# One attention layer with a feed-forward block on one core: two accumulation groups in one PSUM tile, group norm over 512 columns, and a due time for every instruction of the plan

## The chip, the core and the metric

The kernel runs on one core of one Trainium2 chip, in one launch, all in float32. The metric is device time in microseconds. Of the kernel before, three runs are known: 1293.23, 1293.79 and 1300.29 us, median 1293.79 us. TensorE is PE in the profile (PEld is its loading of weights), VectorE is DVE, ScalarE is ACT, GpSimd is POOL, and SP is the engine whose queue issues nearly all DMAs.

## The reference, cut to what matters

One layer on 1024 tokens of width 1024. Four mixers of 256 columns each write the 16 groups of 64 columns; then a norm per group, the output projection and a gated feed-forward block.

```python
def hybrid_layer(x, ...):
    hn = rms_norm(x, g_mix)
    proj = hn @ w_in
    ...
    o_a = nsa_mixer(qa, kca, vca, ksa, vsa, kwa, vwa, gta, b_gate, ...)
    o_b = short_conv_mixer(cvb, cvc, cvu, conv_w).reshape(b, s, CONV_CH // HEAD_DIM, HEAD_DIM)
    o_c = stick_breaking_attention(to_heads(qc, N_HEADS_C), to_heads(kc, N_HEADS_C), to_heads(vc, N_HEADS_C))
    ...
    for window, dil in DILATED_CONFIGS:
        o_i, lse_i = dilated_attention(qdh, kdh, vdh, window, dil, slopes_d)
    ...
    groups = jnp.concatenate([o_a, o_b, o_c, o_d], axis=2)
    groups = rms_norm(groups, g_out.reshape(N_GROUPS, HEAD_DIM)).reshape(b, s, MIX_WIDTH)
    x = x + groups @ w_out
    h2 = rms_norm(x, g_ffn)
    return x + (jax.nn.silu(h2 @ w_gate) * (h2 @ w_up)) @ w_down
```

## The kernel before

Every float32 operand is split into a rounded part and a rest (names ending in h and l, `whi` and `wlo`), and each product is three float32r matmuls (`mm3`, lines 241 to 243): high by high, high by low, low by high.

**Stages.** Input norm, transposes and the first projections; then, as the list `ORDER` names them, the three-branch attention `attn_nsa` for two pairs of heads (`n0`, `n1`), the convolutions (`c0`, `c1`), stick-breaking attention (`proj_stick`, `attn_stick`: `ps`, `s`) and dilated attention (`proj_dil`, `attn_dil`: `pd`, `d`) for two pairs of heads each, the gains (`g`), the output projection (`out_half`), the second norm (`ln2`), and the feed-forward block with Strassen-Winograd products: seven products a step for gate and up (`winograd`, lines 1054 to 1056), then seven for the down projection (lines 241 to 243 with `hw`). In the trace the input norm and the first projections fill the time to some 100 us, attention and projections that to 600 us, gate and up 636 to 1074 us.

**What the change touches.** Attention takes 128 queries of both heads of a pair (`attn_nsa`, tile `qt`), or 256 queries of one head at a time (`pv_heads`, pair `qp`). The weights of a score tile are transposed on PE into a bank `Tp` (line 570), copied by ACT (`pth`, line 558), their rest taken by DVE (`ptl`, line 559), and multiplied with the values on PE into a bank `Op` (lines 575, 576, 694, 695). `Op` holds 512 columns, of which one head or one query tile uses 256. `o_evac` moves it out: ACT copies 64 of its partitions (line 580), DVE adds the other 64 into the tile `MO` (line 582). When `MO` has 256 columns, `finish` norms them: squares (ACT, line 593), their rounded part (ACT, 605) and rest (POOL, 607), two matmuls that sum the squares of each group (PE, 606 and 608), Ln and Exp (ACT, 609 and 610) and the product (DVE, 611); then `MO` is stored (line 617), or, for the last pair of heads, split with its gain (`gain`, lines 819 and 820) into `MH` and `ML`, which `out_half` multiplies.

**Projections beside them.** `v_T` copies a finished projection out of its bank (ACT, `vraw`, line 367) and transposes it on PE (line 370). `normed` copies projections into `raw` (ACT, line 357), scales them (DVE, line 299) and lets PE transpose them (line 343). `q_split` and `k_split` write the halves of queries and keys (lines 311, 312, 319, 321).

**What sets the order.** The kernel is built twice. After the first time a planner (`make_plan`, `_traced`, `_planned`) goes through the instructions like a list scheduler: at each engine, of those that are ready it takes the one with the lowest number, where the number is the place in the program less a lead. Leads come from two tables, `EARLIER` by kind of tile and `LEADS` by group and stage (some 500 entries). The second time the instructions get the planned order on each engine (`fix_order`) and each tile the planned buffer. The plan reaches up to the first use of the pool `f2`, that is to the down projection. Of PSUM's eight banks three are `PR`, two `T`, two `SP`, one `O`; gate and up use all eight in turn (`PF`).

## Time and profile before

| | |
|---|---|
| median of three runs | 1293.79 us |
| the profiled execution, its own time | 1296.53 us |
| its span, first to last instruction | 1294.5 us |
| busy: PE, PEld | 1270.6 us (98%), 1088.3 us (84%) |
| busy: DVE, ACT, POOL | 972.0 us (75%), 701.5 us (54%), 652.2 us (50%) |
| mean granted clock of PE | 0.997 |

The profiled execution took 2.7 us more than the median; 2.0 us of its time lie around the span. A busy PE in this profile is a matmul between its start and a modelled end, and matmuls overlap, so the busy share alone does not say how fast PE goes: the distance from one start to the next does.

### The profile page before, as it was taken

The numbers are of one execution on the slowest core, as the hardware profiler recorded it, in microseconds if no ns is written. First come the engines' busy times: TensorE is split into PE (matmuls) and PEld (weight loads), VectorE is DVE, ScalarE is ACT, GpSimd is POOL, SyncE is SP. The second block draws the span as 40 slices with busy tenths as digits, with TensorE's granted clock in tenths as the row PEclk, the third lists the DMA queues.
The fourth block names the chain that finished last, engine by engine and source line by source line (L and its number), as shares of the span: only waits on it lengthen the run. The fifth ranks groups of instructions, "written<-read, shape, count | busy, mean of one in ns | idle before, by whom it ended". The sixth has DMA issues, their size and how long they took to land.

```text
span 1294.5 us, 20254 instructions
## 1 busy us (share of the span) xinstructions
PE 1270.6 (98%) x7041; PEld 1088.3 (84%) x7041; DVE 972.0 (75%) x1793; ACT 701.5 (54%) x1437; POOL 652.2 (50%) x490
## 2 busy tenths in 40 slices
PE   8999999999999999999999999999999999999998
PEld 8988888888889798999888888888888888887886
DVE  6758878789888979754688896776576667599862
ACT  6557686778889878456553323333232335423540
POOL 6354364445546534434773444444444435565655
PEclk9999999999999999999999999999999999999999
DMA  6340030211111315543554444323313339852534
GB/s 238 110 131 1 9 105 10 61 53 44 55 47 32 97 26 191 165 148 105 194 177 146 155 161 149 123 85 119 122 65 117 103 106 355 277 181 65 146 100 153
DMA packets 90550, 153.04 MB, mean 118 GB/s; under 512 B 10128, under 2 KB 35728, under 8 KB 90448
## 3 DMA queue, kind: packets, MB, share of 16 engines
q1 hardware_dynamic: 89888, 149.92, 36.0%
q0 software_dynamic: 560, 1.84, 0.4%
q8 instruction: 55, 0.90, 0.3%
q14 instruction: 47, 0.39, 0.1%
HBM read 111.08 MB, written 36.44 MB: 114 GB/s over the span
## 4 chain that ended last, share of the span: by engine, by line
PE 59%; DVE 5%; issue 1%; DMA 0%; ACT 0%; POOL 0%; SPq 0%; DVEq 0%; ACTq 0%
PE PRp L241 6%; PE PRp L243 6%; PE PRp L242 6%; PE PRp L1054 4%; PE PRp L1055 4%; PE PRp L1056 4%; PE Tp L1054 2%; PE SPp L1054 2%; PE Tp L1055 2%; PE Tp L1056 2%; PE SPp L1056 2%; PE SPp L1055 2%; DVE bB L1033 2%; PE Tp L570 1%; DVE fw L1114 1%; PE Op L1054 1%
## 5 line engine op out<-in xcount | busy, mean ns | idle before, releaser
L108 POOL TENSOR_TENSOR wlo<-raw,whi 128x512 fp32r<-128x512 f32 x94 | 124.8, 1336 | 102.2 <-ACT whi L107 74.4
L1043 POOL TENSOR_TENSOR fw<-fraw,fw 128x512 fp32r<-128x512 f32 x50 | 71.0, 1421 | 144.4 <-ACT fw L1042 135.4
L559 DVE TENSOR_TENSOR ptl<-Tp,pth 128x512 fp32r<-128x512 f32 (+2 forms) x172 | 102.1, 606 | 25.3 <-ACT pth L558 23.3
L558 ACT ACTIVATE pth<-Tp 128x512 fp32r<-128x512 f32 (+2 forms) x172 | 89.6, 531 | 54.2 <-PE Op L575 24.0
L1114 DVE TENSOR_TENSOR fw<-sraw,fw 128x512 fp32r<-128x512 f32 x73 | 90.5, 1255 | 34.5 <-ACT fw L1113 34.3
L1042 ACT ACTIVATE fw<-fs 128x512 fp32r<-128x512 f32 x88 | 52.0, 629 | 108.2 <-DVE fs L1033 74.1
L1114 POOL TENSOR_TENSOR hw<-bB,hw 128x512 fp32r<-128x512 f32 x55 | 80.8, 1481 | 50.1 <-ACT hw L1113 49.5
L241 PE MATMUL PRp<-XH,whi 128*128 128x512 f32 x224 | 91.4, 408 | 0.0
L242 PE MATMUL PRp<-XL,whi 128*128 128x512 f32 x224 | 90.1, 402 | 0.0
L243 PE MATMUL PRp<-XH,wlo 128*128 128x512 f32 x224 | 89.9, 402 | 0.1
L570 PE MATMUL Tp<-ident,S 128*128 128x128 f32 x552 | 87.6, 273 | 0.0
L1043 DVE TENSOR_TENSOR fw<-fs,fw 128x512 fp32r<-128x512 f32 x88 | 75.1, 880 | 7.6 <-ACT fw L1042 7.5
L107 ACT ACTIVATE whi<-raw 128x512 fp32r<-128x512 f32 x102 | 63.2, 620 | 31.4 <-PE PRp L242 9.3
L651 POOL TENSOR_SCALAR S<-S,ll 128x640 f32<-128x640 f32 (+7 forms) x32 | 53.6, 1675 | 51.9 <-DVE ll L649 30.9
L1042 ACT ACTIVATE fw<-fraw 128x512 fp32r<-128x512 f32 x50 | 31.5, 630 | 84.1 <-DMA fraw<-in_wup_dram 26.3
L570 PEld LDWEIGHTS Tp<-ident,S 128*128 128x128 f32 x552 | 66.6, 140 | 8.3 <-DVE ptl L559 0.2
L241 PE MATMUL PRp<-whi,MH 128*128 128x256 f32 (+1 forms) x248 | 72.0, 293 | 0.9 <-DVE VD L374 0.8
L242 PE MATMUL PRp<-wlo,MH 128*128 128x256 f32 (+1 forms) x248 | 70.9, 287 | 0.0
L243 PE MATMUL PRp<-whi,ML 128*128 128x256 f32 (+1 forms) x248 | 70.6, 287 | 0.0
L1113 ACT ACTIVATE hw<-bB 128x512 fp32r<-128x512 f32 x62 | 38.9, 628 | 49.9 <-PE Op L243 21.2
L1033 DVE TENSOR_TENSOR fs<-fraw 128x512 f32<-128x512 f32 x44 | 42.1, 956 | 31.9 <-DMA fraw<-in_wgate_dram 18.3
L793 POOL TENSOR_TENSOR S<-S,R 128x128 f32<-128x128 f32 (+7 forms) x32 | 47.3, 1483 | 35.7 <-DVE R L791 28.6
(481 smaller groups left out, 4467.5 us busy)
## 6 DMA issues: line engine op xcount, KB each, us to landing
fraw<-in_wgate_dram SPq DMA_DIRECT2D x22, 512.0 KB, 4.2
fraw<-in_wup_dram SPq DMA_DIRECT2D x22, 512.0 KB, 4.1
bB<-in_wdown_dram SPq DMA_DIRECT2D x44, 256.0 KB, 4.5
sraw<-hS SPq DMA_DIRECT2D x44, 256.0 KB, 2.7
raw<-in_wout_dram SPq DMA_DIRECT2D x30, 256.0 KB, 2.8
hS<-s SPq DMA_DIRECT2D x30, 256.0 KB, 2.0
sraw<-hA SPq DMA_DIRECT2D x29, 256.0 KB, 3.6
xt<-in_x_dram SPq DMA_DIRECT2D x8, 512.0 KB, 9.5
```

What stands on the lines that cost most here:

```text
L108: (lo or nc.gpsimd).tensor_tensor(dst_lo, raw, f(dst_hi), op=OP.subtract)
L241: nc.tensor.matmul(ps, a[0], b[0], start=first, stop=False)
L242: nc.tensor.matmul(ps, a[0], b[1], start=False, stop=False)
L243: nc.tensor.matmul(ps, a[1], b[0], start=False, stop=last)
L558: nc.scalar.activation(ph[:, c], tp[:, :n], AF.Copy)
L559: nc.vector.tensor_tensor(pl[:, c], tp[:, :n], f(ph[:, c]), op=OP.subtract)
L570: nc.tensor.transpose(tp[:, i * 128:(i + 1) * 128], p, ident)
L1043: eng.tensor_tensor(wt[:, 1, :], a, f(wt[:, 0, :]), op=OP.subtract)
L1054: nc.tensor.matmul(ps, wt[:, 0, c], bh[:, k, :], start=k == 0, stop=False)
L1055: nc.tensor.matmul(ps, wt[:, 0, c], bl[:, k, :], start=False, stop=False)
L1056: nc.tensor.matmul(ps, wt[:, 1, c], bh[:, k, :], start=False, stop=k == 3)
L1114: eng.tensor_tensor(wt[:, 1, :], raw, f(wt[:, 0, :]), op=OP.subtract)
```

## The change

Two heads (`pv_heads`) or two query tiles (`attn_nsa`) now share one `Op` tile, with `c0` or `oc` as the column where each begins; only the first matmul in the tile carries the flag that starts an accumulation. `o_evac` copies 512 columns once. `MO` holds 512 columns, and `finish` runs once for 512. The temporary of `o_evac` and `finish` (`otmp`) is one buffer of 512 columns where it was two of 256. `EARLIER` and `LEADS` are gone: a table `DUE` gives each of the 9372 planned instructions a number of its own, and the planner takes the ready instruction with the lowest.

```diff
-    def pv(o, items, first=True, last=True):
+    def pv(o, items, first=True, last=True, c0=0):
...
-                nc.tensor.matmul(o[:, 256 - b:256], v, ph[:, c], start=first and g + i == 0, stop=False)
-                nc.tensor.matmul(o[:, 256 - b:256], v, pl[:, c], start=False, stop=last and g + i == n - 1)
+                nc.tensor.matmul(o[:, c0 + 256 - b:c0 + 256], v, ph[:, c], start=first and g + i == 0, stop=False)
+                nc.tensor.matmul(o[:, c0 + 256 - b:c0 + 256], v, pl[:, c], start=False, stop=last and g + i == n - 1)
 
     def o_evac(o, writes):
-        tmp = sm.tile([128, 256], F32, tag="otmp", bufs=2, name="otmp")
-        nc.scalar.activation(tmp[64:128, :], o[64:128, :256], AF.Copy)
-        for dst, c0, c1 in writes:
-            nc.vector.tensor_tensor(dst, o[0:64, c0:c1], tmp[64:128, c0:c1], op=OP.add)
+        tmp = otmp("ok")
+        nc.scalar.activation(tmp[64:128, :], o[64:128, :], AF.Copy)
+        for dst, at in writes:
+            nc.vector.tensor_tensor(dst, at(o)[0:64], at(tmp)[64:128], op=OP.add)
+
+    def otmp(name):
+        return sm.tile([128, 512], F32, tag="otmp", bufs=1, name=name)
 
     def mixtile():
-        return sm.tile([128, 256], F32, tag="MO", bufs=2, name="MO")
+        return sm.tile([128, 512], F32, tag="MO", bufs=2, name="MO")
...
         for qt in range(NT):
+            if qt % 4 == 0:
+                MO = mixtile()
             if qt % 2 == 0:
-                MO = mixtile()
+                o = Ot()
+            oc = qt % 2 * 256
...
             if qt % 2:
-                finish(hp, qt * 128 - 128, 256, MO, tk())
+                mv = MO[:, qt % 4 * 128 - 128:qt % 4 * 128 + 128].rearrange("p (j n) -> p j n", n=128)
+                o_evac(o, [(mv[h * 64:(h + 1) * 64], lambda z, h=h: z.rearrange("p (j g n) -> p j g n", j=2, g=2)[:, :, h, :])
+                           for h in range(2)])
+            if qt % 4 == 3:
+                finish(hp, qt * 128 - 384, 512, MO, otmp("fk"))
...
     def pv_heads(P, V, qp, k8):
-        MO = mixtile()
+        if qp % 2 == 0:
+            MIX["o"] = mixtile()
+        MO = MIX["o"]
+        o = Ot()
         for h in range(2):
-            o = Ot()
...
-            pv(o, items)
-            o_evac(o, [(MO[h * 64:(h + 1) * 64, :], 0, 256)])
-        finish(k8, qp * 256, 256, MO, tk())
+            pv(o, items, first=h == 0, last=h == 1, c0=h * 256)
+        mc = slice(qp % 2 * 256, qp % 2 * 256 + 256)
+        o_evac(o, [(MO[h * 64:(h + 1) * 64, mc], lambda z, h=h: z[:, h * 256:h * 256 + 256]) for h in range(2)])
+        if qp % 2:
+            finish(k8, qp * 256 - 256, 512, MO, otmp("fk"))
...
-EARLIER = {"evac": 1000, "split": 400, "fill": -30, "T": 0, "SP": 10, "O": 150}
-LEADS = {
-    "ACT B22 B": -649,
...
+DUE = """
+-15229 98 85 94 562 -9495 -117 269 -399 538 -348 185 -252 -78 -17 159 -192 37 587 -462 238 51 -277 439 -255 447
...
-        op.lead = sum(EARLIER[k] for k in op.kinds)
-        if acc:
-            op.lead += LEADS.get(op.group, 0) + LEADS.get(op.stage, 0)
...
+    due = list(accumulate(map(int, DUE.split())))
+    due += range(10 ** 8, 10 ** 8 + n - len(due))
...
-                heappush(now[e], (i - ops[i].lead, i))
+                heappush(now[e], (due[i], i))
```

The order on PE, first around the values' projection of the second pair of heads in stick-breaking attention. `PRp` is the projection's bank, `vraw` its copy by ACT, which lines 370 transpose; before:

```order
L242 MATMUL PRp_5876<-XL_139,whi_5872 128x512
L243 MATMUL PRp_5876<-XH_138,wlo_5873 128x512
L241 MATMUL PRp_5876<-XH_138,whi_5872 128x512
L242 MATMUL PRp_5876<-XL_139,whi_5872 128x512
L243 MATMUL PRp_5876<-XH_138,wlo_5873 128x512
L370 MATMUL PRp_5903<-ident_77,vraw_5901 128x128 x4
L522 MATMUL SPp_5427<-ckl_4771,cql_4769 128x512
L524 MATMUL SPp_5427<-ckr_4772,zq_4196 128x512
L241 MATMUL PRp_5910<-XH_140,whi_5866 128x512
```

The transposes stand right behind the projection whose copy they read. The same place now (`PRp_5727` takes the part of `PRp_5903`):

```order
L576 MATMUL Op_5125<-ptl_5183,VC_4637 128x256
L575 MATMUL Op_5125<-pth_5182,VC_4637 128x256
L522 MATMUL SPp_5798<-dkh_5396,dqh_5394 128x128
L576 MATMUL Op_5125<-ptl_5183,VC_4637 128x256
L524 MATMUL SPp_5798<-dkr_5398,zq_4098 128x128
L570 MATMUL Tp_5275<-ident_77,S_5206 128x128
L370 MATMUL PRp_5727<-ident_77,vraw_5725 128x128
L241 MATMUL PRp_5734<-XH_140,whi_5690 128x512
L370 MATMUL PRp_5727<-ident_77,vraw_5725 128x128 x3
```

Products with the values, scores and a transpose were moved in between. Next the group norm of the last store, where dilated attention's first pair of heads ends and the output projection runs beside it (`PRp` from `MH`, `ML`); `pth` and `ptl` are the two parts of the squares. Before:

```order
L241 MATMUL PRp_7563<-whi_7553,MH_6853 128x256
L242 MATMUL PRp_7563<-wlo_7554,MH_6853 128x256
L243 MATMUL PRp_7563<-whi_7553,ML_6854 128x256
L606 MATMUL Tp_6465<-pth_6466,blk1r_130 128x256
L608 MATMUL Tp_6465<-ptl_6467,blk1r_130 128x256
L522 MATMUL SPp_7115<-dkh_6478,dqh_6476 128x512
```

Now (the two matmuls are lines 609 and 611):

```order
L609 MATMUL Tp_6249<-pth_6250,blk1r_130 128x512
L241 MATMUL PRp_7328<-whi_7289,MH_6637 128x256
L241 MATMUL PRp_7351<-whi_7283,MH_6637 128x256
L242 MATMUL PRp_7351<-wlo_7284,MH_6637 128x256
L243 MATMUL PRp_7351<-whi_7283,ML_6638 128x256
L241 MATMUL PRp_7351<-whi_7283,MH_6637 128x256
L242 MATMUL PRp_7351<-wlo_7284,MH_6637 128x256
L522 MATMUL SPp_6879<-dkl_6263,dql_6261 128x512
L524 MATMUL SPp_6879<-dkr_6264,zq_4098 128x512
L242 MATMUL PRp_7328<-wlo_7290,MH_6637 128x256
L611 MATMUL Tp_6249<-ptl_6251,blk1r_130 128x512
```

Nine matmuls stand between the two of the norm, where none stood. Last a place in gate and up, where `PRp_9341` takes the bank that `PRp_9147` leaves, once DVE has read it. Now:

```order
L1065 MATMUL PRp_9147<-B22_8403,fw_9144 128x512
L1066 MATMUL PRp_9147<-B22_8403,fw_9144 128x512
L1064 MATMUL Op_9290<-T4_8402,fw_9287 128x512
L1065 MATMUL Op_9290<-T4_8402,fw_9287 128x512
L1064 MATMUL PRp_9324<-T2_8400,fw_9321 128x512
L1066 MATMUL Op_9290<-T4_8402,fw_9287 128x512
L1064 MATMUL Op_9290<-T4_8402,fw_9287 128x512
L1064 MATMUL PRp_9341<-T1_8399,fw_9338 128x512
```

Before, at such a place (`PRp_9405` takes the bank of `PRp_9238`, whose last matmul stands 69 rows further up, and none of the rows between writes that bank):

```order
L1054 MATMUL PRp_9386<-T3_8659,fw_9383 128x512
L1055 MATMUL PRp_9386<-T3_8659,fw_9383 128x512
L1056 MATMUL PRp_9386<-T3_8659,fw_9383 128x512
L1054 MATMUL PRp_9405<-B22_8661,fw_9402 128x512
L1055 MATMUL PRp_9405<-B22_8661,fw_9402 128x512
```

Five matmuls stand between the last in a bank and the first of the next tile in it. Over gate and up the order has 136 such turns; the fewest matmuls in one were 36 before, and now ten turns have nine or fewer. Bank `O` in attention turns 24 times instead of 48; the fewest matmuls in a turn are 17 now and were 9.

## Rows read from the trace of the kernel before

**Rows 1.** From the page: busy time, share of the span and instructions of each engine.

```profile
PE 1270.6 (98%) x7041; PEld 1088.3 (84%) x7041; DVE 972.0 (75%) x1793; ACT 701.5 (54%) x1437; POOL 652.2 (50%) x490
```

**Rows 2.** Busy time of each engine in stretches of the span; the first number is the length of the stretch, the numbers in brackets count instructions, then the granted clock, the DMA share and GB/s.

```profile
400.00:450.00 50.00, 46.25 (x317) 41.12 (x316) 47.12 (x78) 43.38 (x81) 30.41 (x17) 1.00 0.27 74
...
500.00:550.00 50.00, 46.56 (x353) 43.81 (x352) 39.20 (x93) 31.17 (x70) 25.30 (x19) 1.00 0.44 134
...
630.00:1090.00 460.00, 459.96 (x1996) 370.92 (x1996) 342.82 (x428) 171.40 (x303) 213.44 (x152) 1.00 0.42 141
1090.00:1200.00 110.00, 108.48 (x458) 86.72 (x457) 91.47 (x90) 44.11 (x79) 64.49 (x41) 0.98 0.58 187
```

**Rows 3.** The same view for two short stretches with matmuls of 256 columns and one with 512 columns alone.

```profile
82.60:86.19 3.59, 3.59 (x17) 3.59 (x18) 3.25 (x9) 2.93 (x7) 2.20 (x2) 0.54 0.26 75
86.35:88.87 2.52, 2.52 (x23) 2.52 (x22) 1.13 (x3) 0.38 (x1) 2.52 (x3) 1.00 0.36 104
700.00:800.00 100.00, 100.00 (x430) 80.50 (x429) 83.96 (x104) 34.47 (x60) 45.35 (x30) 1.00 0.48 163
```

**Rows 4.** For whom PE waited between 110 and 600 us, the whole list: total us, times, longest.

```profile
PE PRp L370 <- ACT vraw L367: 2.3, 4, 0.7
PE SPp L522 <- DVE dql L312: 1.6, 1, 1.6
PE Tp L608 <- POOL ptl L607: 1.4, 2, 0.8
PE PRp L241 <- DVE VD L374: 1.1, 2, 0.8
PE PRp L241 <- ACT raw L357: 0.8, 1, 0.8
PE SPp L522 <- DVE S L785: 0.8, 1, 0.8
PE SPp L522 <- PE PRp L243: 0.5, 1, 0.5
PE Op L576 <- DVE ptl L559: 0.5, 2, 0.3
PE PRp L606 <- ACT sh L605: 0.4, 1, 0.4
```

**Rows 5.** PE's instructions in order of time around one of these waits: start, duration, and in brackets the idle time before.

```profile
361.86 0.39 PE L243 MATMUL PRp<-XH,wlo 128*128 128x512 f32 x1
362.94 0.66 PE L370 MATMUL PRp<-ident,vraw 128*128 128x128 f32 x4 [0.69 <-ACT vraw L367]
```

**Rows 6.** The same view around a group norm and behind it.

```profile
515.50 0.38 PE L606 MATMUL Tp<-pth,blk1r 128*128 128x256 f32 x1
516.72 0.39 PE L608 MATMUL Tp<-ptl,blk1r 128*128 128x256 f32 x1 [0.84 <-POOL ptl L607]
...
520.16 0.28 PE L243 MATMUL PRp<-whi,ML 128*128 128x256 f32 x1
522.03 0.47 PE L522 MATMUL SPp<-dkl,dql 128*128 128x512 f32 x1 [1.59 <-DVE dql L312]
```

**Rows 7.** ACT's groups of instructions: out<-in, shape, count, busy us, mean ns.

```profile
L580 ACT ACTIVATE otmp<-Op 64x256 f32<-64x256 f32 x48 | 18.3, 380 | 15.4 <-PE Op L576 14.3
...
L609 ACT ACTIVATE tk<-Tp,epst 128x256 f32<-128x256 f32 x24 | 11.3, 471 | 4.1 <-PE Tp L608 3.8
...
L610 ACT ACTIVATE tk<-tk 128x256 f32<-128x256 f32 x24 | 9.9, 414 | 0.3
...
L593 ACT ACTIVATE tk<-MO 128x256 f32<-128x256 f32 x24 | 9.8, 409 | 6.8 <-DVE MO L582 6.7
...
L294 ACT ACTIVATE sq<-raw 128x512 f32<-128x512 f32 x12 | 7.5, 628 | 0.9 <-PE Tp L343 0.8
...
L311 ACT ACTIVATE dql<-PRp,gsc 64x512 fp32r<-64x512 f32 x4 | 2.7, 683 | 0.1
L609 ACT ACTIVATE yc<-PRp,epst 128x512 f32<-128x512 f32 x4 | 2.7, 682 | 0.1
```

**Rows 8.** DVE's groups, in the same columns.

```profile
L1043 DVE TENSOR_TENSOR fw<-fs,fw 128x512 fp32r<-128x512 f32 x88 | 75.1, 880 | 7.6 <-ACT fw L1042 7.5
L559 DVE TENSOR_TENSOR ptl<-Tp,pth 128x512 fp32r<-128x512 f32 x104 | 70.5, 688 | 21.1 <-ACT pth L558 19.7 <-PE Op L575 0.3 <-PE SPp L522 0.2
...
L582 DVE TENSOR_TENSOR MO<-Op,otmp 64x256 f32<-64x256 f32 x32 | 13.4, 417 | 5.3 <-ACT otmp L580 4.3
...
L1033 DVE TENSOR_TENSOR u<-Tp,u 128x512 f32<-128x512 f32 x18 | 12.4, 690 | 19.9 <-PE Tp L1056 17.7 <-POOL p L1033 2.0
...
L611 DVE TENSOR_TENSOR MO<-MO,tk 128x256 f32<-128x256 f32 x24 | 10.3, 429 | 2.8 <-ACT tk L610 2.8
...
L582 DVE TENSOR_TENSOR MO<-Op,otmp 64x128 f32<-64x128 f32 x32 | 9.1, 284 | 1.1 <-ACT otmp L580 0.2
```

**Rows 9.** The chain of work that ended last, from 433 to 440 us: start, us, what.

```profile
433.67 4.25 DVE R L791
...
439.47 0.39 PE PRp L241
```

**Rows 10.** PE's instruction at the start of the slow stretch of rows 3, in the columns of rows 5.

```profile
82.60 0.39 PE L241 MATMUL PRp<-wa,XH 128*128 128x256 f32 x1 [1.15 <-ACT raw L357]
```

**Rows 11.** For whom SP's queue of DMAs waited, one row of the list: total us, times, longest.

```profile
SPq L617 <- DVE MO L611: 97.6, 11, 35.4
```

More of the change, by code (lines that the diff above doesn't have):

```diff
@@ L621, in flush_stores @@
             nc.sync.dma_start(*stores.pop(0))
-    def tk():
-        return sm.tile([128, 256], F32, tag="otmp", bufs=2, name="tk")
     def attn_nsa(hp, Q):
@@ L693, in attn_nsa @@
             ph, pl = evac_T(tp, 256)
[L694 to L695 removed]
+            nc.tensor.matmul(o[:, oc:oc + 256], vcHL, ph[:, :256], start=qt % 2 == 0, stop=False)
+            nc.tensor.matmul(o[:, oc:oc + 256], vcHL, pl[:, :256], start=False, stop=False)
             five = [(j0, 384, 384), (j0 + 384, 256, 256)]
[L697 removed]
+            pv(o, branch(1, ks, five if CK and qt == 4 else chunks(0, L), False, False), first=False, last=False, c0=oc)
             wch = chunks(0, L) if qt < 4 else five
[L699 to L701 removed]
+            pv(o, branch(2, kw, wch, qt >= 4, False), first=False, last=qt % 2 == 1, c0=oc)
             if qt % 2:
[L703 removed]
+                mv = MO[:, qt % 4 * 128 - 128:qt % 4 * 128 + 128].rearrange("p (j n) -> p j n", n=128)
[3 more added lines that the diff above has]
+                finish(hp, qt * 128 - 384, 512, MO, otmp("fk"))
+    MIX = {}
     def pv_heads(P, V, qp, k8):
[L706 removed]
+        if qp % 2 == 0:
+            MIX["o"] = mixtile()
+        MO = MIX["o"]
+        o = Ot()
         for h in range(2):
[L708 removed]
             items = []
@@ L1235 @@
 PE_RATE = 0.92
[L1236 removed]
+REUSES = {"sd": ("sa",), "bp": ("sm", "sa", "sd"), "lp": ("sm", "sa", "sd"), "lq": ("sm", "sa", "sd"), "b2": ("lq",)}
 PINNED_UNTIL = "f2"
[L1238 to L1764 removed]
@@ L1767, in _size @@
+DUE = """
[302 rows of a table added]
+"""
 def _size(ap):
@@ L1946, in _planned @@
     from heapq import heappush, heappop
+    from itertools import accumulate
     n = len(ops)
```

532 lines of the change are left out of this document (removed), and 301 rows, old and new, of the table DUE.

## The prediction

> **What bounds the kernel now.** I first read the page's busy times: PE is busy 1270.6 us of the span [rows 1]. Since a busy PE need not be a PE at its pace, I next read the stretches. Gate and up hold 430 matmuls of 512 columns in 100.00 us [rows 3]: one every 0.2326 us, and over 460 us no idle time worth a number [rows 2]. There is nothing to win in that third of the time, only to lose. Attention is different: PE is idle 3.75 us between 400 and 450 and 3.44 between 500 and 550, where DVE is busy 47.12 and 39.20 of 50 us [rows 2]. The list of PE's waits says for whom [rows 4]: 15 waits, 9.4 us, on copies by ACT (`vraw`, `raw`), on the rest of the squares by POOL, on DVE.
>
> The view undercounts. From the matmul at 361.86 to the transpose at 362.94 pass 1.08 us, of which 0.2326 are the matmul's pace; 0.85 is lost, and the view shows 0.69 [rows 5]. The missing 0.16 is what a matmul is shown beyond its pace (0.39 against 0.23 us). So the 15 waits lose 9.4 + 15 x 0.16 = 11.8 us, and a wait under 0.16 us isn't in the list at all. Last I read the chain: at 433.67 it lies 4.25 us in DVE's scan `R`, and goes through DVE until PE goes on at 439.47 [rows 9]. PE's waits there end with DVE's queue.
>
> So the end is set by PE's work, which the change leaves as it is (24 norm matmuls fewer, each of twice the columns), plus PE's waits in attention. The gain can only come out of those, 11.8 us and the short ones.
>
> **Copies and norms, part by part.** ACT: the copy out of `Op` was 48 x 0.380 us = 18.2; now 24 of 64x512, by the row of that shape 0.683 each, 16.4. A norm was 0.409 twice (the square; the rounding is of that shape too) + 0.471 + 0.414 = 1.70 us on ACT, 24 times, 40.9; now 12 times 0.628 (square, rounding and, as the nearest row, Exp) x 3 + 0.682 (Ln) = 2.57, together 30.8 [rows 7]. ACT gets 11.9 us back. DVE: the 32 adds of 64x128 at 0.284 become 16 at 0.417, 9.1 to 6.7; the 24 norm products of 0.429 become 12 of 512 columns, between 0.688 and 0.880 by the nearest rows, 10.3 to 8.3 or 10.6 [rows 8]. DVE gets 2.1 to 4.4 us back. Neither engine is the bound on average, so these microseconds count only where PE waits for that engine.
>
> The single `otmp` adds a dependence: the copy out of the next `Op` tile waits until the norm before it is through with its temporary. Behind that copy ACT's later copies `pth` would be queued, and PE waits for those. I cost it at nothing: the norm's chain on ACT, DVE and POOL is some 4 us, and now a whole `Op` tile of two heads or two query tiles is filled before the next copy is due. If that cover is gone, it costs what is left of those 4 us at up to 12 norms.
>
> Bank `O` now waits for one copy of 0.683 and two adds of 0.417, 1.5 us, 24 times, before it was 0.380 + 0.417 = 0.8, 48 times [rows 7, 8]. The whole list of PE's waits has no `otmp` and no `MO` [rows 4], so this move was covered; the order now has at least 17 matmuls in such a turn, where it had 9. Cost 0. The Trainium skill speaks against this part (Perfetto Trace Analysis, Matmuls): independent groups should rotate through different banks so that moving one out overlaps the next one's matmuls. By that rule, uncovered, one bank for both heads would add 24 x 1.5 = 36 us. The trace doesn't agree: one bank turned 48 times without a wait of PE's, since PE has projections to do meanwhile; I give that case no chance of its own.
>
> SP: 20 stores of `MO` become 10 of twice the size. Its queue stood 97.6 us behind such stores [rows 11], with loads queued after them. There are half as many of them now, and PE waited for no load in attention [rows 4]: cost 0; a load that came late would stand among PE's waits or DVE's.
>
> **The order, wait by wait.** Each wait of rows 4 with its hidden 0.16, and what the new order does there (PE work between two rows of the order is counted at the paces of rows 3):
> - `vraw`: 2.3 + 4 x 0.16 = 2.9 us. Five of the eight copies had under 0.6 us of PE work between projection and transposes (none at the first place shown); now one has none, one has 0.7 and six more than that. One wait of 0.85 stays: gain 2.1.
> - `ptl` of the norm (line 608): 1.4 + 0.3 = 1.7. At 515.50 and 516.72 the two matmuls stood one behind the other, 1.2 us apart [rows 6]; now nine stand between. Gain 1.7.
> - `VD`: 1.1 + 0.3 = 1.4. PE work between grows from 0.6 and 1.1 us to 1.5 and 2.4. Gain 1.4.
> - `raw`: 0.8 + 0.16 = 1.0. From none and 0.4 us of work to 0.7 and 0.8. Gain 0.8.
> - `dql`: 1.6 + 0.16 = 1.8, at 520.16 to 522.03 [rows 6]. It came last in a full DVE queue. The score no longer stands so close, but that queue is no shorter in the new order. Half: 0.9.
> - `S`, `PRp`, the other `ptl` and `sh`: 2.2 + 0.8 = 3.0 us. For `S` the order has the same few matmuls; I leave the others too.
>
> Together 6.9 us.
>
> **Short waits.** No row shows them. At least nothing goes; at most PE gets every microsecond that ACT and DVE save, 11.9 + 4.4 = 16.3. The chain in the bad stretch runs over DVE [rows 9], so the nearest rows are DVE's: its saving of 2.1 to 4.4. I take 3.0.
>
> **Gate and up.** Ten turns of a bank now have nine matmuls or fewer in between, five in the case shown; 36 was the least. After the last matmul DVE has to read the bank: 0.16 + 0.690 = 0.85 us, and five matmuls last 1.16. If DVE is free at that moment, nothing is lost; if it has just begun a rest `fw` (0.880) [rows 8], PE waits 0.85 + 0.88 - 1.16 = 0.57. So 0 to 5.7 us for ten. Below nothing it cannot go, PE has no wait to lose there [rows 2]. DVE has been idle before such reads (17.7 us in front of 18 of them [rows 8]), so I take the low side: 1.1. The queue behind a late DVE is its own next rests, for which PE has a stock of weights.
>
> The down projection keeps its order; its stall and slow clock in 1090 to 1200 (1.52 us idle, clock 0.98 [rows 2]) stay.
>
> **Sum.** -6.9 - 3.0 + 1.1 = -8.8 us. Against the profiled execution's own time 1296.5 - 8.8 = 1287.7; the median stands 2.7 us lower, so 1285.0.
>
> **Rivals.**
> - *The waits only change their place*: DVE binds. For it: DVE at 47.12 of 50 us [rows 2], the chain over the scans, only 2.1 to 4.4 us of relief; in the new order two pairs of scores near the end of attention follow a pair with hardly a matmul between, though they want a bank that DVE must read. Against it: 8 of the 15 waits are on ACT and POOL, where the relief is. The 3.0 of short waits don't come and half of the 6.9 comes back: 1296.5 - 3.5 + 1.1 - 2.7 = 1291.4, between 1288 and 1298.
> - *Slower through gate and up*: a late DVE at the tight turns delays PE, and since PE is at 100% there every delay stays. At 0.57 us each it doesn't decide; it does from about 1.5 us each over the ten, where DVE is two instructions late. PE's clock then adds to it: at 82.60, after an idle time of 1.15 us, the granted clock is 0.54 on average, 17 matmuls take 3.59 us, where 23 take 2.52 afterwards (1.2 against 2.4 GHz) [rows 3, 10]; that cost 3.59 - 17 x 0.11 = 1.7 us. Ten turns at 1.5 and four such stretches are 15 + 7 = 22: 1296.5 - 9.9 + 22 - 2.7 = 1305.9. Against it: at 522.03 PE had idled 1.59 us and the clock of that stretch stayed 1.00 [rows 2, 6]. The Trainium skill (TensorE: Matmul & The Clock Gate, HAM oscillation) says that an engine that idles falls back to the lower clock; the trace agrees at 82.60 and not at 522.03.
> - *All of it comes*: the margins in the order do away with the 3.0 that I leave and with more short waits, 6 to 9 us of them. 1296.5 - 9.9 - 9 + 0 - 2.7 = 1274.9.
>
> **How the numbers follow.** My forecast (gain 5 to 14 us, 1280 to 1288.5) has 0.45, all of it 0.15, changed places 0.28, slower through gate and up 0.12. A difference under 0.5%, 6.5 us, can't be told from none: faster means below 1287.3, slower above 1300.3. Faster: 0.38 of the first, 0.15 of the second, 0.53. Same: 0.07 of the first, 0.28 of the third and 0.02 of the fourth, which need not reach its whole price: 0.37. Slower 0.10. The range runs from 1275, where the second case ends, to 1298, the upper end of the third; outside lie most of the fourth and a tail below, under 0.2.
>
> **What would show it.** In the profile of the changed kernel: the list of PE's waits between 110 and 600 us without `ptl` of the norm and `VD` and with one or two `vraw`, its total from 9.4 to under 5; idle time of PE in 400 to 550 well under 7.3 us; in gate and up 430 matmuls in 100 us still, or fewer if the turns are late, with waits of PE for DVE `u`; ACT's time down by some 12 us, DVE's by 2 to 4. I am wrong if the waits in attention go and the time doesn't: then it was lost in gate and up or in waits too short for the view; and if the same sum of waits stands under other names, DVE was the bound.

## The result, and the profile after

The changed kernel takes 1283.11 us (median of five runs, 1281.58 to 1285.18); beside it the kernel before took 1294.98 (five runs). The ratio is 0.990, with a 95% interval of 0.9875 to 0.9929: the kernel got faster by 11.9 us, about 1%. The forecast was 1285.0. The profiled execution took 1281.58 us, with a span of 1279.7; that of before 1296.53 with 1294.5, so the two traces differ by 14.8 us.

The page first: busy time, share of the span and instructions of each engine, as in [rows 1].

```profile
PE 1263.0 (99%) x7017; PEld 1081.8 (85%) x7017; DVE 961.7 (75%) x1763; ACT 689.2 (54%) x1363; POOL 655.4 (51%) x478
```

PE has the same columns to go through, in 24 matmuls fewer. ACT has 12.3 us less work, DVE 10.3 less.

Where the 14.8 us went is read from the starts of three matmuls: the first of gate and up's seven-product steps (line 1054, now 1064), the first of the down projection (with `hw`), and the last. Some plain products of gate and up stand ahead of the first border, from 636.68 us before and 624.42 after; they take 48.3 and 48.4 us, so they have no part in the gain. PE's instructions in order of time, in the columns of [rows 5], before:

```profile
684.98 0.40 PE L1054 MATMUL PRp<-T,fw 128*128 128x512 f32 x1
...
1082.26 0.40 PE L241 MATMUL PRp<-hw,fw 128*128 128x512 f32 x1
...
1189.94 0.49 PE L241 MATMUL Tp<-hw,fw 128*128 128x512 f32 x1 [0.41 <-ACT hw L1113]
1191.55 0.50 PE L242 MATMUL Tp<-hw,fw 128*128 128x512 f32 x1 [1.11 <-POOL hw L1114]
...
1290.02 0.40 PE L243 MATMUL Tp<-hw,fw 128*128 128x512 f32 x1
```

The same view after (the first two rows belong to an experiment below):

```profile
401.43 0.50 PE L609 MATMUL Tp<-pth,blk1r 128*128 128x512 f32 x1 [0.39 <-ACT pth L608]
...
402.40 0.39 PE L241 MATMUL PRp<-whi,XH 128*128 128x256 f32 x1
...
672.82 0.50 PE L1064 MATMUL PRp<-T,fw 128*128 128x512 f32 x1 [0.19 <-ACT fw L1052]
...
1070.42 0.40 PE L241 MATMUL PRp<-hw,fw 128*128 128x512 f32 x1
...
1178.63 0.50 PE L242 MATMUL Tp<-hw,fw 128*128 128x512 f32 x1 [0.71 <-POOL hw L1124]
...
1275.57 0.39 PE L243 MATMUL Tp<-hw,fw 128*128 128x512 f32 x1
```

| stretch | before | after | difference |
|---|---|---|---|
| start to gate and up's steps | 684.98 | 672.82 | -12.2 |
| gate and up's steps, to the down projection | 397.28 | 397.60 | +0.3 |
| down projection, to the last matmul's start | 207.76 | 205.15 | -2.6 |
| the end | 4.5 | 4.1 | -0.4 |

Part of this, in two places, is the granted clock. The windows of the kernel before, in the columns of [rows 2], with the stretch of attention up to 400 us on top:

```profile
100.00:400.00 300.00, 297.06 (x1844) 260.43 (x1843) 249.99 (x724) 234.61 (x540) 151.53 (x120) 1.00 0.15 42
...
82.87:86.28 3.41, 3.41 (x18) 3.41 (x18) 3.07 (x8) 2.66 (x7) 2.29 (x2) 0.50 0.28 79
1192.20:1195.61 3.41, 3.41 (x10) 2.63 (x9) 3.41 (x3) 1.90 (x4) 3.41 (x3) 0.50 0.26 77
```

and after:

```profile
100.00:400.00 300.00, 299.73 (x1888) 264.96 (x1887) 257.84 (x718) 233.70 (x511) 155.34 (x117) 1.00 0.15 42
400.00:450.00 50.00, 48.77 (x342) 43.94 (x340) 42.36 (x83) 41.28 (x75) 27.86 (x14) 1.00 0.28 79
...
500.00:550.00 50.00, 47.60 (x369) 44.83 (x368) 44.14 (x103) 32.28 (x62) 18.68 (x14) 1.00 0.49 156
630.00:1090.00 460.00, 459.81 (x1989) 370.04 (x1988) 329.44 (x418) 173.79 (x303) 216.91 (x150) 1.00 0.41 141
...
82.51:86.10 3.59, 3.59 (x30) 3.59 (x31) 3.49 (x9) 3.08 (x9) 2.77 (x2) 1.00 0.23 73
```

Before, the clock stood at its lower level, 1.2 GHz, for 3.41 us at 82.87 and again at 1192.20; each cost 3.41 x 0.5 = 1.7 us. After, there is none: at 82.51 PE starts 30 matmuls in 3.59 us, where it started 17 [rows 3]. So of the 12.2 us ahead of gate and up 1.7 are clock and 10.5 are work, and of the 2.6 us in the down projection 1.7 are clock and 0.9 a shorter stall: there the weights `hw` came late for two matmuls in a row, now for one. Traces of one and the same order in that stage differ by up to 0.7 (experiment 5), so these 0.9 are hardly more than chance. In their clock the two profiled executions differ by more than the two kernels do: over the 66 runs of before that were taken beside the experiments the mean granted clock is 0.9981, over the five runs of after 0.9992. By that some 0.0011 x 1290 = 1.4 us of the 11.9 are clock, an estimate.

In attention PE's idle time fell from 3.75 to 1.23 us between 400 and 450, and from 3.44 to 2.40 between 500 and 550 [rows 2]. For whom PE waited between 110 and 600 us, the whole list after the change, in the columns of [rows 4]:

```profile
PE PRp L243 <- DVE ML L830: 0.7, 1, 0.7
PE PRp L241 <- DVE dkr L321: 0.7, 1, 0.7
PE Tp L570 <- DVE S L766: 0.7, 1, 0.7
PE PRp L370 <- ACT vraw L367: 0.7, 1, 0.7
PE Tp L570 <- DVE ptl L559: 0.6, 2, 0.4
PE SPp L522 <- DVE mm L549: 0.5, 1, 0.5
PE Tp L609 <- ACT pth L608: 0.4, 1, 0.4
```

Eight waits, 4.3 us, where 15 took 9.4. The norm's `ptl`, `VD`, `raw` and `dql` are gone, `vraw` is down from four to one. The last windows show something else: between 100 and 400 us DVE did 249.99 us of work before and 257.84 after, and between 400 and 450 it is busy for 42.36 us where it was for 47.12 [rows 2].

The wide instructions after the change, ACT's and then DVE's groups, in the columns of [rows 7, 8]:

```profile
L580 ACT ACTIVATE ok<-Op 64x512 f32<-64x512 f32 x24 | 14.2, 593 | 10.7 <-PE Op L576 10.3
L612 ACT ACTIVATE fk<-Tp,epst 128x512 f32<-128x512 f32 x12 | 8.2, 686 | 4.1 <-PE Tp L611 3.8
...
L582 DVE TENSOR_TENSOR MO<-Op,ok 64x256 f32<-64x256 f32 x48 | 20.0, 417 | 2.8 <-ACT ok L580 1.6
...
L614 DVE TENSOR_TENSOR MO<-MO,fk 128x512 f32<-128x512 f32 x12 | 8.3, 693 | 5.5 <-ACT fk L613 5.4
```

The copy took 0.593 us where 0.683 was reckoned, Ln 0.686 (0.682 reckoned) and the product 0.693, at the low end of its range. The copy `ok` was kept waiting by PE's matmuls (10.3 us), not by the norm that uses the one temporary before it.

### The profile page after: what moved, and what is told of

It is laid out like the page before. It is cut to its first block, busy times and chain, and to the rows that moved or that the text cites. A ratio compares the mean times of both kernels' runs of the same rounds, so it can differ in the third digit from the quotient of the medians.

```text
span 1279.7 us, 20087 instructions
## 1 busy us (share of the span) xinstructions
PE 1263.0 (99%) x7017; PEld 1081.8 (85%) x7017; DVE 961.7 (75%) x1763; ACT 689.2 (54%) x1363; POOL 655.4 (51%) x478
## 4 chain that ended last, share of the span: by engine, by line
PE 55%; DVE 4%; issue 1%; ACT 1%; DMA 1%; POOL 0%; SPq 0%; DVEq 0%; POOLq 0%; ACTq 0%
PE PRp L241 5%; PE PRp L242 5%; PE PRp L243 5%; PE PRp L1064 4%; PE PRp L1066 4%; PE PRp L1065 4%; PE SPp L1064 2%; PE Tp L1064 2%; PE Tp L1065 2%; PE Tp L1066 2%; PE SPp L1066 2%; PE SPp L1065 2%; PE Op L1064 1%; PE Op L1065 1%; PE Op L1066 1%; DVE fw L1124 1%
## 5 line engine op out<-in xcount | busy, mean ns | idle before, releaser
L108 POOL TENSOR_TENSOR wlo<-raw,whi 128x512 fp32r<-128x512 f32 x94 | 130.3, 1393 | 93.2 <-ACT whi L107 71.5
L559 DVE TENSOR_TENSOR ptl<-Tp,pth 128x512 fp32r<-128x512 f32 (+2 forms) x172 | 103.1, 605 | 13.7 <-ACT pth L558 11.8
L1124 POOL TENSOR_TENSOR hw<-bB,hw 128x512 fp32r<-128x512 f32 x55 | 80.8, 1482 | 49.0 <-ACT hw L1123 48.4
L570 PE MATMUL Tp<-ident,S 128*128 128x128 f32 x552 | 98.8, 273 | 1.3 <-DVE S L766 0.7
L570 PEld LDWEIGHTS Tp<-ident,S 128*128 128x128 f32 x552 | 68.7, 140 | 11.3 <-issue 2.1
L243 PE MATMUL PRp<-whi,ML 128*128 128x256 f32 (+1 forms) x248 | 68.0, 289 | 0.7 <-DVE ML L830 0.7
L241 PE MATMUL PRp<-whi,MH 128*128 128x256 f32 (+1 forms) x248 | 67.8, 290 | 0.7 <-DVE dkr L321 0.7
```

The lines of the kernel that those rows point to most:

```text
L108: (lo or nc.gpsimd).tensor_tensor(dst_lo, raw, f(dst_hi), op=OP.subtract)
L241: nc.tensor.matmul(ps, a[0], b[0], start=first, stop=False)
L243: nc.tensor.matmul(ps, a[1], b[0], start=False, stop=last)
L559: nc.vector.tensor_tensor(pl[:, c], tp[:, :n], f(ph[:, c]), op=OP.subtract)
L570: nc.tensor.transpose(tp[:, i * 128:(i + 1) * 128], p, ident)
L1124: eng.tensor_tensor(wt[:, 1, :], raw, f(wt[:, 0, :]), op=OP.subtract)
```

## The experiments

Three things could make the 10.5 us in attention: the matmuls that now stand between a copy and its reader, the time saved on ACT and DVE, or the order as a whole together with the groups. "Wide" and "narrow" below mean the groups of after and of before. Where a kernel is said to keep an order, its plan is not computed but given, instruction by instruction. Lists of PE's waits are in the columns of [rows 4].

**1. Filling PE's waits in the kernel before.** At 12 places PE gets matmuls that are ready in front of the one that waits:

```diff
+MOVES = [
+    (2940, [2284, 2285]),
+    (3310, [3112, 3113, 3114]),
+    (3106, [3115, 3116, 3117]),
...
+    for x, zs in MOVES:
+        for k, z in enumerate(zs):
+            start[z] = start[x] - 1e-3 * (len(zs) - k)
```

> The kernel before, its groups of 256 columns, its rule and its order on ACT, DVE, POOL and SP unchanged. Only on PE, at 12 places between 240 and 520 us where its trace shows PE idle, 35 matmuls that were ready at that moment are moved in front of the waiting one (1 to 4 each, mostly the next projection's). By the trace they cover 6.3 us of idle time. Theory A (the gain comes from what stands between a copy and the matmul that reads it): the covered idle time goes and stays away, the median falls by 5 to 6 us to about 1289.5; the list of PE's waits between 110 and 600 us falls from 9.4 us to about 5. Theory B (the gain comes from the time that the wider instructions save on ACT and DVE; moved matmuls only shift a wait to the next place): the median stays above 1293, the waits come back under other names and the list's sum falls by less than 2 us.

Measured: 1294.35 us (12 runs) against 1295.60 (23 runs); ratio 0.9993, interval 0.998 to 1.0006. Of the 6.3 us of covered idle time 1.2 came off the median, and the interval reaches from a gain of 2.6 to a loss of 0.8. In its own trace PE runs, in order of time:

```profile
436.14 0.39 PE L608 MATMUL Tp<-ptl,blk1r 128*128 128x256 f32 x1 [1.03 <-POOL ptl L607]
...
437.12 0.58 PE L241 MATMUL PRp<-whi,XH 128*128 128x256 f32 x1 [0.48 <-DVE VD L374]
```

PE comes to these two and meets operands that have not become earlier: the norm's `ptl` keeps it for 1.03 us, where the longest such wait was 0.8 [rows 4]. The list of its waits between 110 and 600 us begins so:

```profile
PE Tp L608 <- POOL ptl L607: 1.9, 2, 1.0
PE SPp L522 <- DVE dql L312: 1.6, 1, 1.6
PE PRp L241 <- DVE VD L374: 1.3, 2, 0.8
PE Op L576 <- DVE ptl L559: 1.3, 3, 0.8
```

`vraw` (2.3 us in [rows 4]) is gone, and both kinds of `ptl`, `VD` and (in a row further down) `S` have grown. The whole list sums to 9.5 us, where it was 9.4. Theory A, filling alone, falls; the waits change their place, as B had it. B's other half, that the saved time on ACT and DVE makes the gain, is experiment 4's question.

**2. The same edit in the changed kernel**, three places, 13 matmuls with the same few lines and this list:

```diff
+MOVES = [
+    (3828, [3885, 3886, 3887, 3888]),
+    (4400, [4406, 4407, 4408, 4409]),
+    (4682, [5069, 5070, 5071, 5150, 5072]),
+]
```

> The changed kernel; only on PE, at three of its remaining waits (401.4, 425.3 and 486.7 us), 13 matmuls that were ready are moved in front of the waiting one; they cover 1.7 us. If PE sets the pace here (the transposes put back in the run before cost 1.8 us each and nothing gave it back), the median falls by 1.0 to 1.7 us, to 1281.4 to 1282.1. If the waits come back elsewhere, as with the same edit in the kernel before, it stays at 1283.

Measured: 1283.24 us (four runs), ratio 0.9903 (0.9887 to 0.9920), as without the edit (0.9902). Its trace shows how such a wait moves:

```profile
401.52 0.50 PE L609 MATMUL Tp<-pth,blk1r 128*128 128x512 f32 x1
402.49 0.38 PE L241 MATMUL PRp<-whi,XH 128*128 128x256 f32 x1 [0.47 <-ACT raw L357]
```

In the changed kernel line 609 had waited (401.43, the rows above) and line 241 came at 402.40. Four transposes now fill the time before line 609, and line 241, whose bank ACT has still to read, waits instead. Two neighbours hung on ACT, and only one was seen waiting. The whole list sums to 4.1 us, where it was 4.3.

**3. Putting readers back behind their copies**, in the changed kernel. Again the same lines; each of the seven entries holds the four transposes of one `vraw`:

```diff
+MOVES = [
+    (3169, [3046, 3047, 3048, 3049]),
+    (2695, [3077, 3078, 3079, 3080]),
...
```

> The changed kernel, with only PE's order altered: the transposes of seven of the eight value projections are put back right behind the projection whose copy they read (the eighth stands so already and waits 0.85 us). Theory A: each of the seven waits 0.85 us again, 6 us in all, and nothing gives it back: median about 1289. The list of PE's waits shows vraw 8 times for some 5.5 us where it was once 0.7. Theory B: the waits show, but ACT and DVE, with their saved time, get ahead meanwhile and later waits shrink by as much: median 1283 to 1285.

Measured: 1295.24 us (12 runs), 12.1 us more than the changed kernel (11.3 by the ratios, each to the runs of before beside it), and 6 more than theory A had said; ratio to before 0.9989 (0.9977 to 1.0001). The first place in its trace, and the head of its list of waits:

```profile
302.61 0.48 PE L243 MATMUL PRp<-XH,wlo 128*128 128x512 f32 x1
303.82 0.66 PE L370 MATMUL PRp<-ident,vraw 128*128 128x128 f32 x4 [0.73 <-ACT vraw L367]
```

```profile
PE PRp L370 <- ACT vraw L367: 7.0, 8, 1.5
PE PRp L241 <- DVE VD L374: 2.3, 2, 1.9
```

`vraw` waits 8 times, as expected, but for 7.0 us (7.0 + 8 x 0.16 = 8.3 with the hidden part, against 0.85 for its one wait in the changed kernel: 7.4 more), and `VD`, which DVE writes from those transposes, 2.3 where it had none. The whole list is 12.4 us in 16 waits, where it was 4.3 in eight: 9.4 more with the hidden parts. A mean clock of 0.9977 over its runs against 0.9992 makes some 1.9 us (an estimate), and together that is nearly all of the 12.1. So here nothing is given back; a delay of PE reached its followers too. This alone does as much harm as the whole change does good. It does not contradict the first experiment: there a wait was covered and the next one that hung on the other engines grew by as much; here matmuls were put where their operand is not ready, and what stands behind them came later.

**4. The saved instruction time.** The order, tiles and buffers of the changed kernel, with the wide instructions of ACT and DVE each cut in two:

```diff
-        nc.scalar.activation(tmp[64:128, :], o[64:128, :], AF.Copy)
+        for z in (slice(0, 256), slice(256, 512)):
+            nc.scalar.activation(tmp[64:128, z], o[64:128, z], AF.Copy)
...
-        nc.scalar.activation(tmp, m, AF.Square)
...
+        for z in zs:
+            nc.scalar.activation(tmp[:, z], m[:, z], AF.Square)
...
```

> The changed kernel with its tiles, buffers and order on every engine; only the 512-column instructions of ACT and DVE on these tiles (copy out of the bank, square, rounding, Ln, Exp, the add of two query tiles, the norm's product) are each done as two of half the columns, one right behind the other. By the durations of the kernel before this gives ACT 14 us and DVE 4 us of work back, what the wider instructions save. Theory A: PE's waits lie elsewhere, the median rises by 0 to 2 us, to at most 1285. Theory B: the saved time was the gain, it rises by 8 to 12 us, to 1291 or more, with new waits of PE for the two engines in attention.

Measured: 1282.91 us (four runs), ratio 0.9896 (0.9876 to 0.9916). Nothing is lost. One of its groups:

```profile
L581 ACT ACTIVATE ok<-Op 64x256 f32<-64x256 f32 x48 | 15.6, 374 | 10.4 <-PE Op L576 10.1
```

A half lasts as long as in the kernel before (374 ns, 380 there), but two back to back overlap: 48 take 15.6 us and not 18, and the page gives ACT 694.2 us (5.0 more than after, not 14) and DVE 963.9 (2.2 more). Less time was given back than planned, then, but for this order the answer is clear as far as it goes: 5.0 of ACT's 12.3 us and 2.2 of DVE's 10.3 cost it nothing. The Trainium skill (Perfetto Trace Analysis, Optimizing Scalar/DVE Operations) says that larger operations can raise throughput where the engine is saturated; ACT at 54% and DVE at 75% are not, and the run agrees.

**5. The old order in gate and up.** Each number of the table is now a planned start: up to the second norm the changed kernel's own, from there on that of before's plan. The turns of the banks in gate and up are then those of before, with 36 matmuls at the least in one.

```diff
 DUE = """
--15229 98 85 94 562 -9495 -117 269 -399 538 -348 185 -252 -78 -17 159 -192 37 587 -462 238 51 -277 439 -255 447
...
+0 468 176 292 251 283 109 109 109 109 109 109 109 109 109 109 109 109 109 109 109 109 109 109 109 109 109 109 109 109
...
```

> The changed kernel, with the numbers from the second norm on (gate and up) replaced by the starts of the kernel before's plan, so that gate and up have the old order (fewest matmuls in a turn of a bank 36 instead of 5). In the profiles gate and up took 386.2 us before and 386.5 after (first matmul to last), the down projection behind it 218.9 before and 216.3 after. Theory C (the down projection got shorter because DVE leaves gate and up with less work behind it in the new order): with the old order gate and up stay within 0.5 us of 386.3 and the down projection is back near 218.9, with a stall of about 2 us some 120 us behind its start; median 1285 to 1286. Theory D (it got shorter by chance of the granted clock or through what comes before): the down projection stays near 216.3, median 1283. The prediction's price for the tight turns, 1.1 us, would show as 1 us less in gate and up.

Measured: 1287.17 us (four runs), ratio 0.9928 (0.9908 to 0.9948). PE's first matmuls of gate and up and of the down projection:

```profile
677.63 0.50 PE L1064 MATMUL PRp<-T,fw 128*128 128x512 f32 x1 [0.68 <-ACT fw L1052]
...
1075.14 0.40 PE L241 MATMUL PRp<-hw,fw 128*128 128x512 f32 x1
```

Gate and up take 397.51 us, against 397.28 and 397.60: neither order is better, and the tight turns cost 0.1. (The expectation set the border to the down projection 11.1 us earlier, at the last matmul of line 1056 or 1066.) From 1075.14 to the last matmul at 1280.81 the down projection takes 205.67, against 207.76 and 205.15: it stays near that of after, as theory D has it. The 0.5 us to after can't be put down to the order of gate and up: with the new order there, the traces of experiments 2 and 3 have 205.8 and that of experiment 4 has 205.3. In this trace 4.8 us are lost ahead of 677.63 (672.82 in the changed kernel): with other numbers behind it the planner also set the end of attention otherwise. On PE the two orders part at 473 us. So the run says little on the total (the expectation had 1283 to 1286), but it settles the stretch that it was for. DVE's additions in gate and up show where most of DVE's 10.3 us came from. Before, after, and with the old order again:

```profile
L1033 DVE TENSOR_TENSOR u<-u,u 128x512 f32<-128x512 f32 x22 | 27.5, 1248 | 12.1 <-POOL u L1033 11.8
```

```profile
L1043 DVE TENSOR_TENSOR u<-u,u 128x512 f32<-128x512 f32 x22 | 23.1, 1049 | 5.6 <-POOL u L1043 5.5
```

```profile
L1043 DVE TENSOR_TENSOR u<-u,u 128x512 f32<-128x512 f32 x22 | 28.1, 1277 | 12.1 <-POOL u L1043 11.8
```

The same 22 additions take 0.2 us less each in the new order of gate and up, 4.4 us in all, and PE gained nothing by it. In the other traces their mean lies between 983 and 1081 ns with the new order there, and between 1187 and 1276 with the old one.

**6. Groups and order crossed.** First the wide groups in the old order: the changed kernel's program, with the places of its instructions given (`PLACE`, one per instruction) instead of planned. The merged copies and norms stand where the second narrow ones stood.

```diff
-    ops, first, tags = _traced(_program(tc), pools.marks)
...
+    return list(accumulate(map(int, PLACE.split()))), slots
```

> The changed kernel's tiles and instructions (two heads or query tiles in one bank, group norm over 512 columns), but every engine keeps the order of the kernel before; the merged copy, the adds and the norm of 512 columns stand where the second of the two narrow ones stood. Theory O (the new order makes the gain, the wide groups nothing): the median stays at 1295, up to 2 us more where the merged copy comes late. Theory G (the wide groups relieve ACT and DVE where the old order waited for them, which halving them again in the changed kernel could not show, since its order no longer waits there): 1284 to 1289. Theory J (each is worth something only with the other): 1292 to 1296 here, and nothing gained either with the narrow groups in the new order.

Measured: 1311.53 us (four runs), ratio 1.0121 (1.0099 to 1.0143). Its list of waits between 110 and 600 us begins with PE's wait for the wide norm's squares. In its own order this wait came once, with 0.4 us; here three times:

```profile
PE Tp L609 <- ACT pth L608: 3.9, 3, 2.9
```

In all it has 31 waits and 20.3 us, where the kernel before had 15 and 9.4: 13.5 us more with the hidden parts. A mean clock of 0.9958 over its runs, against 0.9977 over those of before beside it, makes some 2.5 us more (an estimate). Together that is 16.0 of the 16.7 us lost.

Then the reverse, by the same edit in the program before:

> The reverse: the kernel before's tiles and instructions (one head or query tile at a time in the bank, norm over 256 columns), in the changed kernel's order on every engine; the copy of the first head or query tile stands as far behind its last matmul as the merged copy does, and the second one's matmuls behind it. The bank's turns have 5 matmuls or more in between. Theory O: 1283 to 1287, the changed kernel's time plus what PE waits at 24 more turns of the bank (5 matmuls of 256 columns are 0.6 us, copy and add take 0.8, so up to 0.5 us at the tightest few). Theory G: 1294 or more. Theory J: 1290 to 1296, with waits of PE for the copy or the adds (otmp, MO) in its list.

Measured: 1376.13 us (four runs), ratio 1.0635 (1.0597 to 1.0673). Its list of waits between 110 and 680 us (attention lasts longer here) names PE's banks:

```profile
PE Tp L570 <- DVE ptl L559: 22.0, 26, 2.0
PE Op L575 <- DVE MO L582: 12.2, 13, 1.9
```

In these two kernels neither half has a gain of its own; each without the other costs. Theories O and G fall. J is right on the sign, but it had said 1290 to 1296, and the losses are far beyond that.

**7. Which half of the groups the order needs.** The shared bank with narrow norms, and the reverse:

```diff
...
-            if qt % 4 == 3:
-                finish(hp, qt * 128 - 384, 512, MO, otmp("fk"))
+                finish(hp, qt * 128 - 128, 256, MO, otmp("fk")[:, :256])
...
```

> Half of the narrow groups in the new order: two heads or query tiles share the bank as in the changed kernel, but the norm runs over 256 columns, 24 times; the added norms stand as far behind their last matmul as the wide ones do. With both halves narrow the new order took 1376. Theory N (the new order has no room for 24 norms, each takes one of the two banks T and the pair of buffers that the score tiles use): most of the 93 us come here, 1330 or more, and under 1310 with the narrow bank and the wide norm. Theory K (it has no room for 48 turns of bank O): under 1310 here, 1330 or more there.

```diff
-        o = Ot()
         for h in range(2):
+            o = Ot()
             items = []
...
-            pv(o, items, first=h == 0, last=h == 1, c0=h * 256)
...
+            pv(o, items)
+            o_evac(o, [(MO[h * 64:(h + 1) * 64, mc], lambda z: z[:, :256])])
...
```

> The other half: one head or query tile at a time in bank O, 48 turns with 5 matmuls or more in between, the norm over 512 columns, 12 times, in the new order. Theory K (the turns): 1330 or more, with waits of PE for the adds (MO) and the copy of bank O. Theory N (the norms): under 1310. If both take a share, the two runs' losses against 1283 add up to about 93 us.

Measured: 1367.77 us with narrow norms (ratio 1.0557, 1.0524 to 1.0590) and 1311.96 with the narrow bank (1.0131, 1.0110 to 1.0153). The heads of their lists between 110 and 680 us, narrow norms first, with one row of DVE's waits behind PE's:

```profile
PE Tp L570 <- DVE ptl L559: 21.0, 24, 2.0
PE Tp L609 <- ACT pth L608: 10.3, 11, 2.8
...
DVE ptl L559 <- PE Tp L611: 5.4, 5, 2.1
```

and with the narrow bank:

```profile
PE Op L575 <- DVE MO L582: 13.0, 13, 1.8
PE Op L695 <- DVE MO L582: 5.7, 8, 1.0
```

Against 1283.1 that is 84.7 and 28.9 us, together 113.6: the two losses don't add up to the 93 of both halves. It is the norms first, as theory N has it, though the narrow bank came out 2 us above its border of 1310. Each norm takes one of the two banks `T` and one of the two pairs of buffers `pth` and `ptl` that every tile of weights needs too. In the list PE's transposes (line 570) wait 24 times, 21.0 us, for DVE's rest `ptl`, which is the last to read their bank, and that rest itself waited 5.4 us for a norm's matmul (line 611), which reads such a buffer; the changed kernel has no wait of this kind. The single temporary, which is used twelve times more often too, kept the copy `ok` for 0.8 us only. The turns of bank `O` come second, and are now in plain sight: 21 waits, 18.7 us.

**8. Were the narrow ones only put in the wrong place?** The kernel of experiment 6 with narrow groups, with another table of places: the copies, adds and norms at their old distances from their last matmul.

```diff
 PLACE = """
...
-9 16 2 -129 2 8 1 -4 9 1 10 14 2 3 2 66 2 5 13 -3 12 13 8 14 -156 1 7 2 1 6 15 4 20 5 21 -16 45 2 7 8 29 1 -136 6 1 1
+5 11 -1 12 14 14 19 -13 28 4 2 1 4 10 19 7 3 2 -129 1 10 1 4 15 -1 12 13 3 31 -25 38 1 2 3 10 18 -6 16 1 1 8 7 8 2 3 5
...
```

> Narrow groups in the new order once more, with one thing altered against the run that took 1376: the copies, adds and norms stand as far behind their last matmul as they did in the kernel before, not as far as the wide ones do. If those 81 us came from where the added instructions were put (a norm that stands late holds a bank T, and the tiles behind it in that bank), most of them go: 1283 to 1300, and the new order is worth its gain with narrow groups too. If the order has no room for the narrow groups wherever they stand, 1330 or more.

Measured: 1362.80 us (four runs), ratio 1.0512 (1.0495 to 1.0530): 13 us better than 1376, and still 80 behind the changed kernel. Their places make 13 of the 93 us.

**9. An order searched anew for the other two pairs.** Wide groups with the old rule, `DUE` gone and other leads:

```diff
...
-            heappush(now[e], (due[i], i))
+            heappush(now[e], (i - ops[i].lead, i))
```

> The changed kernel's groups, but the rule of the kernel before: no number per instruction, the place in the program less a lead by kind, group and stage, with the leads searched anew for the wide groups (557 of them). Theory T (the number per instruction makes the gain): 1290 or more. Theory F (the wide groups make it, with any order that is fitted to them): 1281 to 1286, and PE's waits between 110 and 600 us again around 5 us.

The narrow groups with a table, in place of `EARLIER` and `LEADS`:

```diff
...
-            heappush(now[e], (i - ops[i].lead, i))
+            heappush(now[e], (due[i], i))
```

> The narrow groups of the kernel before with the other half of the change, a number for every instruction, begun at the old order and searched for these groups with the planner's own durations. Theory T (a number per instruction makes the gain, whatever the groups): 1283 to 1289. Theory J (it makes it only with the wide groups): 1293 to 1297. The wide groups with the old rule and leads searched in the same way took 1302; if this run is above 1297 too, such a search doesn't carry over to the chip, and neither run says what the rule or the table could reach.

Measured: 1301.66 us for the wide groups with leads (10 runs, ratio 1.0041, 1.0029 to 1.0052), 1296.97 for the narrow ones with a table (12 runs, ratio 1.0008, 0.9997 to 1.0018). Neither gains. By the numbers theory T is right on the first (the table is needed) and J on the second (the table needs the wide groups). But these orders are only as good as the search behind them, and the first came out slower than the kernel before, though it was fitted to its groups; some 2.6 us of its loss lie in gate and up's steps, which take 399.86 us in its trace against 397.28, away from the groups. Neither run says what the rule, or a table for narrow groups, could reach.

## Why the prediction was right, and where its reasons were not

*The sum.* A change of -8.8 us was forecast. Between the two profiled executions it is -14.95, between the medians -11.9. Of the 6.2 us between the forecast and the profiled executions, 3.4 are the two half-clock stretches, which the prediction let stay; the terms below make up the rest.

*Wait by wait.* -6.9 was forecast for the named waits. With 0.16 for each they fell from 11.8 to 4.3 + 8 x 0.16 = 5.6, by 6.2. `vraw`, `ptl`, `VD` and `raw` went as listed; `dql` went whole, not half, and new waits on DVE, for `ML` and `dkr`, came instead. The size is right. The reason given, that matmuls now stand between producer and reader, is half of it: experiment 3 shows that taking them out costs 12.1 us, and experiment 1 that putting them in, on PE alone, brings 1.2 and at most 2.6. This is the step that failed as an explanation: the waits were counted as if each were PE's alone, but in the traces of experiments 1 and 2 the next matmul that hung on ACT, DVE or POOL waited in their place. That a wait goes only where the other engine's chain gets earlier too fits this, but was not tried by itself; what the trace of the changed kernel shows of it is DVE, with 7.9 us more work done between 100 and 400 us.

*Short waits.* -3.0 was taken, from DVE's saving. Attention won 10.5 without the clock, 6.2 of it in named waits, so 4.3 came from short ones and the first 110 us. The size is near, but by luck as far as the runs show: it was taken from DVE's saved time, and giving ACT and DVE part of the saved time back cost nothing (experiment 4).

*ACT and DVE.* ACT's saving was 12.3 us, as reckoned (11.9). DVE's was 10.3 instead of 2.1 to 4.4; the groups gave 13.4 + 9.1 + 10.3 - 20.0 - 8.3 = 4.5 of it [rows 8], and additions in gate and up, by their order alone (experiment 5), 4.4 more (the additions shown).

*Costs set at nothing.* The single `otmp`: no copy waited for a norm. The stores: PE's list has no wait for a load. Bank `O`: PE's list has no wait for it either. But the sentence on the Trainium skill (Perfetto Trace Analysis, Matmuls) set the rule on rotating banks aside too lightly. With narrow turns in the new order PE waited 18.7 us for that bank: in this kernel the rule holds where the order of the other work does not cover the turn; with wide groups the new order does cover it.

*Gate and up.* +1.1 was taken, from 0 to 5.7; it is +0.3 between the two traces, and +0.1 against the old order in experiment 5. The rival that went slower there did not happen: PE started 1989 matmuls in 460 us, as before (1996), without a wait worth a number.

*The down projection* was said to stay as it is; between the two traces 0.9 us of its stall went, and 1.7 of clock.

*The rival of changed places* describes what an edit to PE alone did (experiments 1 and 2). For this change, which moves all engines, it did not come: the list fell from 9.4 to 4.3 us.

What stays open: which engine's part of the new order makes the gain, and whether another search would find as good an order for the narrow groups. The first wasn't tried by itself; the second was tried with one kind of search.

## What to carry to other kernels

Don't count a wait as won because something ready can be put in front of it: look at the next instructions too. Where they hang on the other engines' chains, filling one wait moved it to them here. A wider group can be worth more than the instruction time that it saves, where each group passes through a scarce bank or buffer: here giving 5 us of that time back cost nothing, while 12 more norms through two banks and two pairs of buffers cost 85 us, clock included, in an order without room for them. An order and the groups that it was made for belong together: here either alone lost, so measure them together.

## What the runs showed that was not expected

The lower clock comes and goes at one place with the same instructions: the kernel before had it at 82.87 us in its profiled execution, after a wait of 1.15 us for `raw` [rows 10]. With the moves of experiment 1, which change nothing on PE ahead of 240 us, that wait was 1.10 us and the clock stayed up. There it fell at 436.93, behind the waits shown above, and at 522.27, behind a wait of 1.57 us for `dql`; the kernel before had waited 1.59 us for it at full clock. The windows of that trace:

```profile
82.87:86.28 3.41, 3.41 (x31) 3.41 (x30) 3.03 (x9) 2.77 (x7) 2.56 (x2) 1.00 0.31 89
436.93:440.34 3.41, 3.22 (x15) 3.22 (x16) 2.44 (x6) 2.66 (x7) 2.74 (x2) 0.50 0.40 102
522.27:525.68 3.41, 3.41 (x15) 3.23 (x16) 2.08 (x10) 1.18 (x3) 0.46 (x1) 0.50 0.85 295
```

Each stretch at the lower clock costs 1.7 us, so single profiles of one kernel can differ by that much with the same instructions. In the kernels with many waits the mean clock over the runs fell as low as 0.979 (narrow norms, experiment 7), so that some 29 us of those 1368 are clock, an estimate: (1 - 0.979) x 1368. The Trainium skill (TensorE: Matmul & The Clock Gate, HAM oscillation) has an engine that pauses fall back to the lower clock; its example has longer pauses than the waits here. Over the runs the three kernels with the most waits (experiments 6 and 8 and the narrow norms) had the lowest clock, 0.979 to 0.990, which agrees, though no single wait here tells whether the clock will fall.

DVE's additions of one shape, 128 x 512 from SBUF to SBUF, took 1248, 1049 and 1277 ns on the mean in three kernels with the same program in that stage, and the last two differ in its order (experiment 5).
